# TensorE in program order for the gated delta rule's and the attention's small products, in few groups

## The chip, the cores and the metric

The kernel runs on one core of a Trainium2 chip. The metric is the device time of one execution, in microseconds (us): 2460.8 us before, the median of three runs.

## What is computed

The reference is a two-layer trunk on x of 256 tokens by 2048 channels in fp32. Layer one mixes tokens with a gated delta rule of 16 heads in chunks of 64, layer two with differential attention of 8 heads; each is followed by a feed-forward block (FFN) with a causal convolution of its gate.

```python
# layer 1: projections, convolution, rule, gated norm, output projection
proj = h @ w_in                                   # q, k, v, z, and the gates b, a
qkv = silu(causal_dwconv(proj[..., :o_qkv], conv_w))
beta = sigmoid(b); g = -exp(a_log) * softplus(a + dt_bias)
# in each chunk of 64: decay = exp(g_i - g_j), lower = (beta k) k^T * decay (strictly lower)
sol = triangular_solve(lower, [v * beta, kb * exp(g)], unit_diagonal=True)
# state carried over the chunks; o = q*exp(g) @ state + (q k^T * decay) @ v_new
return (rmsnorm(o, norm_w) * silu(z)) @ w_out
# layer 2: per head two score maps, masked softmax, a = p0 - lam * p1, o = a @ v, rmsnorm, @ w_o
# FFN: (silu(causal_dwconv(gate) + bias) * up) @ w_down
```

## The kernel before

**Large products.** Each fp32 weight block of 128 x 1024 numbers is loaded by SyncE's queue into a tile raw, and split into a high part hi (ScalarE, L219) and a low part lo (VectorE, L220), so that TensorE can take both as fp32r. Such a block is called a half here. Where the weights are stationary (`wstat`: k, q, v heads, FFN, attention's q and k), TensorE runs pairs: hi against 512 columns (L241) and lo against 256 (L242), 8 pairs a half. Where x is stationary (`xstat`, `xstat_steps`: the gate z, w_out, attention's v and w_o, the FFN's second matrix) it runs three products of 512 columns for each of two k blocks and two token tiles (L318 to L320). raw, hi and lo have four buffers each. Four PSUM buffers (mm) hold large results, four (ax) small ones.

**Small products** stand between the large ones:
- gates and decays (`gates_and_decays`): a transpose of the gates (bgT), then for each quarter of the heads three products d1, d2, d3 of 512 columns (L711, L713, L715), whose exponentials ScalarE writes into the tiles ma1 and ma2;
- key products kk (L614, L615) of each head, which VectorE multiplies into ma and reduces to the norms ssk (L618 to L620); from all 16 heads' norms comes cc (L547 to L549), which is transposed (cT_ps, L555). GpSimd then inverts 128 units of 32 x 32 (`eliminate`) and writes them to DRAM (ut_d, un_d), from where 14 copies of 64 KB bring them into the tiles T128 (named t in the trace; L769, L772);
- query products kq and transposes qt (L627 to L632);
- `merge` builds the inverse of 128 x 128 from the 32 x 32 units: 64 products iw, 96 ix, 64 iy (L792, two records of the trace each). `wstat` takes one group of four of them from the list `side` after each k block (`beside`, SMALL = 4);
- rule heads (`head`, `head_end`): per head a chain of transposes and products with ScalarE, VectorE and GpSimd between (L852 to L885), two heads under way;
- attention: scores, transposes of the weights at, products with v (po), transposes aot of the outputs.

**What sets the order.** The program gives each engine's instructions an order in code; the Tile scheduler then orders each engine's queue by its own plan. SyncE's queue and the three compute engines stand in written order only where `manual_schedule` is named (the entry of each block: `in_order`). In the delta rule and the attention TensorE's order is the scheduler's.

Of the kernel before, what the change touches and what calls it, by code (L numbers as in the profile page):

```python
# [15 lines left out]
P = 128  # L16
# [6 lines left out]
AH = 8  # L23
# [9 lines left out]
KEY_LAG, MERGE_AT, HOME_AT = 8, 11, 8  # L33
SMALL = 4
# [68 lines left out]

class Trunk:
    def __init__(self, nc, tc, a, out, cst, stp, bigp, resp, tmp, mmp, axp, scr):
        self.nc, self.tc, self.a, self.out = nc, tc, a, out
        self.cst, self.stp, self.bigp, self.resp, self.tmp = cst, stp, bigp, resp, tmp
        self.mmp, self.axp, self.scr = mmp, axp, scr
        self.due, self.ahead, self.side = [], [], []
# [113 lines left out]
    def wstat(self, srcs, xT, name, early=0):  # L223
# [4 lines left out]
        for hf in range(2):  # L228
# [3 lines left out]
            for k, tt in todo:  # L232
# [10 lines left out]
                self.beside()  # L243
        return ps

    def beside(self):

        if self.side:
            self.side.pop(0)()

    def wstats(self, srcs, xT, first, name):

        for o in self.wstat([srcs[i] for i in range(first)], xT, f"{name}_f", EARLY):
# [211 lines left out]
    def gdn(self):  # L465
# [35 lines left out]
        beta = self.gates_and_decays(gate, ma1, ma2, szt)  # L501
# [9 lines left out]
        late = []  # L511

        def lagging(lag, most, fn, *args):

            late.append((fn, args))
            for _ in range(most):
                if len(late) > lag:
                    f, x = late.pop(0)
                    f(*x)

        def drain():
            while late:
                f, x = late.pop(0)
                f(*x)

        def key_products(h):
            self.key_products(h, K, MA1, MA2, g)
            if h % 4 == 3:
                self.units_out(h // 4, ma1, ma2)
# [6 lines left out]
        z = self.xstat_steps(Blocks(a["w_in"], 48), KD, xT, evac_z, "z")  # L536
        for h in range(NH):
# [11 lines left out]
        nc.vector.tensor_tensor(cc, cc, beta, op=ALU.mult)  # L549
# [14 lines left out]
        self.eliminate(cT, T128, units)  # L564
        self.rsqrt(fl(rb), fl(g["ssk"]), 1.0)
        nc.gpsimd.tensor_tensor(rb, rb, beta, op=ALU.mult)

        for h in range(NH):
            if h == MERGE_AT:
                self.merge(ma1, ma2, cc, T128, units)  # L570
            ps = self.wstat([a["w_in"][h]], xT, f"q{h}")[0]
            qT = self.t([P, S], f"qT{h}", "vT", bufs=3)
            self.conv_silu(qT, ps, h)
            lagging(LAG, 1, self.query_products, h, qT, K, MA1, MA2, g)
            for _ in range(2 - h % 2):
                next(z)
# [4 lines left out]
        vs, heads = [], []  # L581
        for h in range(NH):
            ps = self.wstat([a["w_in"][32 + h]], xT, f"v{h}")[0]
            if h == 0:
                drain()
                self.rsqrt(fl(rq), fl(g["ssq"]), 1.0)
                nc.gpsimd.tensor_scalar(rq, rq, P ** -0.5, None, op0=ALU.mult)
                assert not self.side
            vT = self.t([P, S], f"vT{h}", "vT", bufs=3)
            self.conv_silu(vT, ps, 32 + h)  # L590
            vs.append((h, vT))
            if len(vs) > 1:
                heads.append(self.head(*vs.pop(0), MA1, MA2, T128, negc, rb, rq))
            if len(heads) > 1:
                self.head_end(*heads.pop(0), SZ, oT)
            if h == HOME_AT:
                for tt in range(2):
                    for q in range(4):
                        self.after_halves(tt * 8 + q * 2, lambda tt=tt, sl=slice(q * 512, (q + 1) * 512): nc.sync.dma_start(
                            self.h[:, tt, sl], a["x"][tt * P:(tt + 1) * P, sl]))  # L600
        heads.append(self.head(*vs.pop(0), MA1, MA2, T128, negc, rb, rq))
        for i, x in enumerate(heads):
            self.after_halves(1 + 2 * i, lambda x=x: self.head_end(*x, SZ, oT))
# [18 lines left out]
    def query_products(self, h, q, K, MA1, MA2, g):  # L622

        nc = self.nc
        k, m1, m2 = K[h], MA1[h], MA2[h]
        pp = self.ax(f"kq_{h}")
        nc.tensor.matmul(pp[:, 0:S], k[:, 0:P], q, start=True, stop=True)  # L627
        nc.tensor.matmul(pp[:, S:384], k[:, P:S], q[:, P:S], start=True, stop=True)
        pq = self.ax(f"qt_{h}")
        for p in range(2):  # L630
            qt = pq[:, p * P:(p + 1) * P]
            nc.tensor.transpose(qt, q[:, p * P:(p + 1) * P], self.ident)  # L632
            junk = self.t([P, P], f"jq{h}{p}", "jq")
            nc.scalar.activation(junk, qt, AF.Square, accum_out=g["ssq"][:, p, h:h + 1])
        nc.vector.tensor_tensor(m1[:, 1, :], pp[:, 0:S], m1[:, 1, :], op=ALU.mult)
        nc.vector.tensor_tensor(m2[:, 1, :], pp[:, S:384], m2[:, 1, :], op=ALU.mult)
# [12 lines left out]
    def gates_and_decays(self, ps, ma1, ma2, szt):  # L649
# [22 lines left out]
        xa = self.t([P, S], "ba_xa", "vT", bufs=3)  # L672
# [19 lines left out]
        pt = self.ax("bgT_ps")  # L692
        for p in range(2):
            nc.tensor.transpose(pt[:, p * 64:(p + 1) * 64], bg[0:64, p * P:(p + 1) * P], self.ident[0:64, 0:64])
        bgT = self.cst.tile([P, 2, 64], F32, name="bgT")
        nc.vector.tensor_copy(bgT, pt[:, 0:128].rearrange("p (a c) -> p a c", a=2))
# [3 lines left out]
        for q in range(4):  # L700
# [26 lines left out]
        return bgT[:, :, 0:NH]  # L727
# [14 lines left out]
    def eliminate(self, cT, T128, room):  # L742
# [22 lines left out]
        for p in range(2):  # L765
            for b in range(4):
                u = slice((p * 4 + b) * NH, (p * 4 + b + 1) * NH)
                bs = slice(b * 32, (b + 1) * 32)
                nc.gpsimd.dma_start(T128[p][bs, :, bs], ut[u].rearrange("h c i -> c h i"))  # L769
                if b < 3:  # L770
                    o = (b * 32 + 64) % 128
                    nc.gpsimd.dma_start(T128[p][bs, :, o:o + 32], un[u].rearrange("h i c -> i h c"))  # L772

    def merge(self, ma1, ma2, cc, T128, room):
# [9 lines left out]
        todo = self.side  # L784

        def small(fns):

            for i in range(0, len(fns), SMALL):
                todo.append(lambda part=fns[i:i + SMALL]: [f() for f in part])

        def prod(o, x, y):
            return lambda: nc.tensor.matmul(o(), x(), y(), start=True, stop=True)  # L792

        def quarters(p):
            t = T128[p]
            box = {}

            def begin():
                box[1] = self.ax(f"iw{p}").rearrange("p (h i) -> p h i", h=NH)
                box[2] = self.ax(f"ix{p}").rearrange("p (h i) -> p h i", h=NH)  # L800

            todo.append(begin)
            ws = room[:, p * 512:(p + 1) * 512].rearrange("p (h i) -> p h i", h=NH)
            A, B = (slice(0, 32), slice(64, 96)), (slice(32, 64), slice(96, 128))
            small([
                prod(lambda b=b, h=h: box[1][b, h, :], lambda a=a, b=b, h=h: mt(p, h)[a, b], lambda a=a, h=h, o=o: t[a, h, o:o + 32])
                for h in range(NH) for a, b, o in ((A[0], B[0], 64), (A[1], B[1], 0))])

            def scaled():
                for b in B:  # L810
# [294 lines left out]
```

## Time and profile before

| | us |
|---|---|
| median of three runs (2459.75 to 2467.18) | 2460.8 |
| the profiled execution's own time | 2446.62 |
| its span | 2444.9 |
| TensorE busy in it | 2417.2 |
| VectorE busy | 1654.3 |
| ScalarE busy | 1203.0 |
| GpSimd busy | 148.8 |
| granted TensorE clock, mean | 0.997 |

The profiled execution took 14.2 us less than the median of the timed runs. In the profile the stages follow one another: entry to 45 us, key heads with gates, decays and the first z blocks to 165, query heads with z (and the elimination on GpSimd) to 365, v heads with the rule heads to 495, w_out to 572, FFN to 1300, attention to 1700, FFN to the end. [...]

### The profile page before, as it was taken

How to read it: one execution, taken by the hardware profiler on the slowest of the kernel's cores; microseconds unless marked ns; L12 is line 12 of the kernel's file. 1: busy time of each engine (PE TensorE's matmuls, PEld its weight loads, DVE VectorE, ACT ScalarE, POOL GpSimd, SP SyncE). 2: the span in 40 equal slices, each digit the busy share in tenths (PEclk: the TensorE clock that was granted, in tenths of full speed). 3: DMA queues.
4: the chain of work that ended last, by engine and by line, in shares of the span. 5: the costliest groups of instructions: out<-in, count | busy, mean ns of one | idle time of the engine just before them, and what ended most of it. 6: DMA issues, size and time to landing. Idle time of an engine off the chain costs nothing.

```text
span 2444.9 us, 35002 instructions
## 1 busy us (share of the span) xinstructions
PE 2417.2 (99%) x13203; PEld 2062.2 (84%) x13203; DVE 1654.3 (68%) x2555; ACT 1203.0 (49%) x1940; POOL 148.8 (6%) x237
## 2 busy tenths in 40 slices
PE   9999999999999999999999999999999999999998
PEld 7788778878888888888888888888888888888887
DVE  7777558857877777764446677556777777774444
ACT  6745435545544444444446555444644444444442
POOL 0238201100000000000000000000000000000000
PEclk9999999999999999999999999999999999999999
DMA  6355535444555555565554554455555555555554
GB/s 231 128 176 183 169 113 181 178 159 157 196 190 190 190 190 190 190 209 194 193 195 152 189 185 164 167 189 179 180 190 190 190 189 189 190 195 203 196 193 153
DMA packets 137433, 445.28 MB, mean 182 GB/s; under 512 B 14752, under 2 KB 31952, under 8 KB 136752
## 3 DMA queue, kind: packets, MB, share of 16 engines
q1 hardware_dynamic: 135264, 440.00, 53.1%
q0 software_dynamic: 2000, 3.05, 0.4%
q8 instruction: 103, 1.69, 0.3%
q14 instruction: 66, 0.54, 0.1%
HBM read 439.31 MB, written 3.69 MB: 181 GB/s over the span
## 4 chain that ended last, share of the span: by engine, by line
PE 90%; POOL 3%; issue 2%; ACT 2%; DVE 2%; DMA 1%; SPq 0%; POOLq 0%; DVEq 0%; ACTq 0%
PE ps_up L241 26%; PE ps_up L242 13%; PE ps_d L319 7%; PE ps_d L318 7%; PE ps_d L320 7%; PE ps_v L241 2%; PE ps_ak L241 2%; PE ps_aq L241 2%; PE ps_v L242 1%; PE ps_av L320 1%; PE ps_av L318 1%; PE ps_av L319 1%; PE ps_ao L318 1%; PE ps_ao L319 1%; PE ps_ao L320 1%
## 5 line engine op out<-in xcount | busy, mean ns | idle before, releaser
L241 PE MATMUL ps_up<-xT_f,hi_up 128*128 128x512 f32 x2752 | 955.1, 393 | 0.0
L242 PE MATMUL ps_up<-xT_f,lo_up 128*128 128x256 f32 x2752 | 762.4, 277 | 1.6 <-DVE lo_up L220 1.6
L241 PEld LDWEIGHTS ps_up<-xT_f,hi_up 128*128 128x128 f32 x2752 | 515.9, 187 | 119.0
L219 ACT CAST hi_up<-raw_up 128x1024 fp32r<-128x1024 f32 x344 | 361.1, 1051 | 473.1 <-issue 321.2
L220 DVE TENSOR_TENSOR lo_up<-raw_up,hi_up 128x1024 fp32r<-128x1024 f32 x344 | 421.1, 1225 | 193.7 <-ACT hi_up L219 193.4
L242 PEld LDWEIGHTS ps_up<-xT_f,lo_up 128*128 128x128 f32 x2752 | 516.8, 188 | 3.0 <-DVE lo_up L220 2.7
L220 DVE TENSOR_TENSOR lo_d<-raw_d,hi_d 128x1024 fp32r<-128x1024 f32 x168 | 205.8, 1225 | 223.9 <-ACT hi_d L219 223.9
L219 ACT CAST hi_d<-raw_d 128x1024 fp32r<-128x1024 f32 x168 | 177.1, 1054 | 256.2 <-PE ps_d L320 239.6
L318 PE MATMUL ps_d<-hi_d,hT 128*128 128x512 f32 x672 | 261.4, 389 | 0.0
L320 PE MATMUL ps_d<-hi_d,hT 128*128 128x512 f32 x672 | 261.4, 389 | 0.0
L319 PE MATMUL ps_d<-lo_d,hT 128*128 128x512 f32 x672 | 261.4, 389 | 0.0
L318 PEld LDWEIGHTS ps_d<-hi_d,hT 128*128 128x128 f32 x672 | 126.2, 188 | 26.4
L320 PEld LDWEIGHTS ps_d<-hi_d,hT 128*128 128x128 f32 x672 | 126.1, 188 | 26.3
L319 PEld LDWEIGHTS ps_d<-lo_d,hT 128*128 128x128 f32 x672 | 126.1, 188 | 25.8
L241 PE MATMUL ps_q<-xT_in,hi_q 128*128 128x512 f32 x256 | 97.9, 415 | 0.0
L187 POOL TENSOR_SCALAR qr<-q 128x1 f32<-128x1 f32 x8 | 1.5, 191 | 1578.2 <-DVE q L445 1578.2
L241 PE MATMUL ps_v<-xT_in,hi_v 128*128 128x512 f32 x256 | 93.1, 400 | 0.0
L241 PE MATMUL ps_ak<-xT_kv,hi_ak 128*128 128x512 f32 x240 | 86.8, 402 | 0.0
L901 DVE SCALAR_TENSOR_TENSOR gy<-gs,c_fconv,gy 128x255 f32<-128x255 f32 (+1 forms) x176 | 84.6, 481 | 2.8
L241 PE MATMUL ps_k<-xT_in,hi_k 128*128 128x512 f32 x224 | 81.0, 404 | 0.8 <-DVE s L263 0.8
L646 DVE SCALAR_TENSOR_TENSOR y<-s,c_gconv,y 128x255 f32<-128x255 f32 x144 | 72.2, 502 | 13.9 <-ACT y L644 11.7
L241 PE MATMUL ps_aq<-xT_q,hi_aq 128*128 128x512 f32 x224 | 78.2, 391 | 0.0
(394 smaller groups left out, 4145.0 us busy)
## 6 DMA issues: line engine op xcount, KB each, us to landing
raw_up<-in_w_up SPq DMA_DIRECT2D x344, 512.0 KB, 4.3
raw_d<-in_w_dn SPq DMA_DIRECT2D x176, 512.0 KB, 3.4
raw_z<-in_w_in SPq DMA_DIRECT2D x32, 512.0 KB, 3.9
raw_q<-in_w_in SPq DMA_DIRECT2D x32, 512.0 KB, 3.3
raw_v<-in_w_in SPq DMA_DIRECT2D x32, 512.0 KB, 3.2
raw_wo<-in_w_out SPq DMA_DIRECT2D x32, 512.0 KB, 3.3
raw_av<-in_w_v SPq DMA_DIRECT2D x32, 512.0 KB, 3.3
raw_ao<-in_w_o SPq DMA_DIRECT2D x32, 512.0 KB, 3.2
```

Of the source, the lines that this page charges most:

```text
L187: nc.gpsimd.tensor_scalar(dst, src, scale, EPS, op0=ALU.mult, op1=ALU.add)
L219: nc.scalar.copy(hi[:, c], raw[:, c])
L220: nc.vector.tensor_tensor(lo[:, c], raw[:, c], hi[:, c].bitcast(F32), op=ALU.subtract)
L241: nc.tensor.matmul(to, hi[:, w], x, start=(k == 0 and tt != 1), stop=False)
L242: nc.tensor.matmul(lt, lo[:, w], lx, start=False, stop=(k == KD - 1))
L318: nc.tensor.matmul(to, xh, wh, start=(k == 0), stop=False)
L319: nc.tensor.matmul(to, xh, wl, start=False, stop=False)
L320: nc.tensor.matmul(to, xl, wh, start=False, stop=(k == nk - 1))
L646: nc.vector.scalar_tensor_tensor(y[:, j:S], s[:, 0:S - j], w[:, ct, 3 - j:4 - j], y[:, j:S], op0=ALU.mult, op1=ALU.add)
L901: nc.vector.scalar_tensor_tensor(y[:, j:S], s[:, 0:S - j], w[:, l, f, 2 - j:3 - j], y[:, j:S], op0=ALU.mult, op1=ALU.add)
```

## The change

TensorE's order in the delta rule's heads (`gdn_heads`) and in the attention (`attend_all`) becomes that of the program, by a `manual_schedule` on TensorE alone, and the program is written so that small products stand in few groups:
- bgT after the key head 7, the four quarters of decays around the z blocks of heads 8 and 9, key products of three heads at a time after the z blocks of heads 10 to 14, those of heads 14 and 15 with cT_ps directly behind the query head 0;
- query products of two heads at a time;
- the merge in four runs (iw, ix, two iy), one after each of the query heads 13, 14 and 15 and one at v head 0; the list `side` goes;
- the 14 copies into T128 go from GpSimd's queue to SyncE's, at query head 11 and two halves on;
- a six-stage pipeline of rule heads (class Heads): each step issues one stage of six heads, in three ax buffers; after the last v head six more steps, one half apart, in w_out. The loads of x that are needed again come later for the second token tile;
- attention: scores of a head pair together, the transposes of a head only with the scores of the next, products with v and their transposes for two heads together; the first key head is no longer taken in two token tiles (early 0).

```diff
+    def pe_in_order(self):
+        return self.tc.manual_schedule(engines={mybir.EngineType.PE})
...
-        beta = self.gates_and_decays(gate, ma1, ma2, szt)
+        with self.pe_in_order():
+            self.gdn_heads(gate, ks, xT, ma1, ma2, szt, MA1, MA2, SZ)
+    def gdn_heads(self, gate, ks, xT, ma1, ma2, szt, MA1, MA2, SZ):
+        bg, decays = self.gates_and_decays(gate, ma1, ma2, szt)
...
+        groups = {(7, 0): bg, (8, 0): lambda: decays(0), (8, 1): lambda: decays(1), (9, 0): lambda: decays(2), (9, 1): lambda: decays(3)}
+        for i, hs in enumerate(((0, 1, 2), (3, 4, 5), (6, 7, 8), (9, 10, 11), (12, 13))):
+            groups[10 + i, 1] = lambda hs=hs: key_group(*hs)
         for h in range(NH):
...
             self.conv_silu(K[h], ks[h], 16 + h)
-            lagging(max(1, min(KEY_LAG, 2 * (NH - 1 - h))), 3, key_products, h)
+            groups.get((h, 0), lambda: None)()
             if h >= NH // 2:
                 next(z)
-        drain()
+            groups.get((h, 1), lambda: None)()
+        q0 = self.wstat([a["w_in"][0]], xT, "q0")[0]
+        key_group(14, 15)
...
-        self.eliminate(cT, T128, units)
+        back = self.eliminate(cT, T128, units)
...
         for h in range(NH):
-            if h == MERGE_AT:
-                self.merge(ma1, ma2, cc, T128, units)
+            if h == BACK_AT:
+                back[0]()
+                self.after_halves(2, back[1])
...
+            next(z)
+            if len(late) == 2:
+                self.query_products(late, K, MA1, MA2, g)
+                late = []
+            late.append((h, qT))
+            if h > BACK_AT + 1:
+                next(merge)
+            if h % 2 == 0:
                 next(z)
...
-                nc.gpsimd.dma_start(T128[p][bs, :, bs], ut[u].rearrange("h c i -> c h i"))
+                nc.sync.dma_start(T128[p][bs, :, bs], ut[u].rearrange("h c i -> c h i"))
...
+class Heads:
+    DEPTH = 6
+    def step(self, new):
+        self.under_way = [{"h": new[0], "vT": new[1]} if new else None] + self.under_way[:-1]
+        at = [x for x in enumerate(self.under_way) if x[1]]
+        if not at:
+            return
+        ps = [self.k.ax(f"px{at[0][1]['h']}_{i}") for i in range(3)]
+        room = [ps[0][:, 0:256], ps[0][:, 256:384], ps[0][:, 384:512], ps[1][:, 256:384], ps[1][:, 0:256], ps[2][:, 0:256]]
+        for i, x in reversed(at):
+            (self.turn, self.first, self.across, self.second, self.outputs, self.finish)[i](x, room[i])
...
+        for i in range(pipe.DEPTH):
+            self.after_halves(1 + i, lambda x=last if i == 0 else None: pipe.step(x))
...
-        for c, ps in enumerate(self.wstats(a["w_k"], xkv, 1, "ak")):
+        for c, ps in enumerate(self.wstats(a["w_k"], xkv, 1, "ak", 0)):
             self.add_halves(kq[c][:, 0, :], ps, f"ak{c}")
-            if c % 2 == 1:
-                self.after_halves(2, lambda h=c // 2: self.weights_of(h, kq, aT[h]))
+            if c % 2 == 0 and c > 0:
+                turn()
+                turn = self.weights_of(c // 2 - 1, kq, aT[c // 2 - 1])
```

The three places where the order matters below are shown in rows of each engine's queue. First TensorE at the merge, of the kernel before, in the query head 11: iw products stand in fours behind each pair of large ones (t128 is T128, ma1 the products' tile of the first token tile).

```order
L241 MATMUL ps_q11_0_2834<-xT_in_0_132,hi_q11_0_0_2837 128x512
L242 MATMUL ps_q11_0_2834<-xT_in_0_132,lo_q11_0_0_2838 128x256
L792 MATMUL iw0_2843<-t128_0_1641,ma1_1_386 32x32 x4
L241 MATMUL ps_q11_0_2834<-xT_in_1_151,hi_q11_0_0_2837 128x512
L242 MATMUL ps_q11_0_2834<-xT_in_1_151,lo_q11_0_0_2838 128x256
L792 MATMUL iw0_2843<-t128_0_1641,ma1_1_386 32x32 x4
```

The same products on TensorE of the changed kernel, between the z block that follows query head 13 and query head 14:

```order
L383 MATMUL ps_z_3_1_2798<-hi_z_3_4_3081,xT_in_2_170 128x512
L871 MATMUL iw0_3097<-t128_0_1688,ma1_0_385 32x32 x8
L871 MATMUL iw0_3097<-t128_0_1688,ma1_1_386 32x32 x8
L871 MATMUL iw0_3097<-t128_0_1688,ma1_2_387 32x32 x8
L871 MATMUL iw0_3097<-t128_0_1688,ma1_3_388 32x32 x8
L871 MATMUL iw1_3132<-t128_1_1689,ma2_0_389 32x32 x16
L871 MATMUL iw1_3132<-t128_1_1689,ma2_1_390 32x32 x16
L310 MATMUL ps_q14_0_3167<-xT_in_0_132,hi_q14_0_0_3170 128x512
```

All 64 iw products stand in one run. Counted over the whole order, the 224 products of the merge stood in 48 runs (36 of 32 x 32 products, 12 of 64 x 64) and now stand in 4 (64 iw, 96 ix, 32 iy, 32 iy).

The second place is the transpose cT_ps on TensorE. Before, the last key product (kk_15) stands in the query head 1, and cT_ps 39 rows behind it, after the rest of that head and three quarters of a z block:

```order
L614 MATMUL kk_15_1620<-h_80 128x256
L615 MATMUL kk_15_1620<-h_80 128x128
L242 MATMUL ps_q1_0_1866<-xT_in_0_132,lo_q1_0_0_1870 128x256
...
L320 MATMUL ps_z_1_1_1829<-hi_z_1_2_1937,xT_in_1_151 128x512
L555 MATMUL cT_ps_1644<-ident_81,cc_499 32x128
```

In the changed kernel it is the row behind kk_15, and the z block waits behind it:

```order
L687 MATMUL kk_14_1658<-h_80 128x256
L688 MATMUL kk_14_1658<-h_80 128x128
L687 MATMUL kk_15_1667<-h_80 128x256
L688 MATMUL kk_15_1667<-h_80 128x128
L619 MATMUL cT_ps_1691<-ident_81,cc_429 32x128
L381 MATMUL ps_z_1_0_1816<-hi_z_1_0_1820,xT_in_0_132 128x512
```

VectorE's queue of the changed kernel at that place, where cc is made; it is what cT_ps turns:

```order
L691 SCALAR_TENSOR_TENSOR jd14_1661,ssk_427<-kk_14_1658,ident_81 128x128
L691 SCALAR_TENSOR_TENSOR jd14_1663,ssk_427<-kk_14_1658,ident_81 128x128
L692 TENSOR_TENSOR ma1_3_388<-kk_14_1658,ma1_3_388 128x256
L693 TENSOR_TENSOR ma2_1_390<-kk_14_1658,ma2_1_390 128x128
L289 TENSOR_TENSOR lo_q1_0_1_1880<-raw_q1_0_1_1877,hi_q1_0_1_1879 128x1024
L326 TENSOR_TENSOR s0_1805<-ps_q0_0_1613,c_qkv0_1806 128x256
...
L693 TENSOR_TENSOR ma2_1_390<-kk_15_1667,ma2_1_390 128x128
L328 TENSOR_TENSOR s0_1805<-s0_1805,rb_in_229 128x256
L611 TENSOR_SCALAR cc_429<-ssk_427 128x32
L612 RECIPROCAL cc_429<-cc_429 128x32
L613 TENSOR_TENSOR cc_429<-cc_429,bgT_425 128x32
```

Between the two heads' four operations stand a split of a weight half (lo_q1) and an addition for query head 0 (s0).

## Rows read from the trace of the kernel before

**Rows 1.** The page, part 1: busy time, share of the span and instructions of each engine.

```profile
PE 2417.2 (99%) x13203; PEld 2062.2 (84%) x13203; DVE 1654.3 (68%) x2555; ACT 1203.0 (49%) x1940; POOL 148.8 (6%) x237
```

**Rows 2.** Stretches: start:end, length, busy us of each engine, PEclk, DMA share, GB/s.

```profile
90.00:100.00 10.00, 7.53 (x37) 6.33 (x35) 5.10 (x13) 9.89 (x15) 4.62 (x6) 0.83 0.31 107
250.00:300.00 50.00, 45.85 (x333) 36.45 (x331) 29.34 (x43) 20.91 (x42) 11.65 (x16) 0.93 0.54 174
291.00:298.50 7.50, 4.92 (x63) 4.09 (x64) 1.58 (x5) 1.53 (x4) 1.63 (x3) 0.54 0.22 67
490.00:500.00 10.00, 8.62 (x52) 7.18 (x51) 3.25 (x11) 3.15 (x15) 2.12 (x6) 1.00 0.00 1
500.00:510.00 10.00, 8.53 (x44) 6.18 (x43) 6.20 (x11) 6.89 (x16) 2.12 (x6) 1.00 0.18 57
1500.00:1550.00 50.00, 50.00 (x246) 41.94 (x246) 31.47 (x57) 25.06 (x48) 1.78 (x4) 1.00 0.49 167
```

**Rows 3.** TensorE in order of time, 293 to 298 us: start, length, instruction, [idle before].

```profile
293.58 1.45 PE L792 MATMUL ix<-t,units 32*32 32x32 f32 x46 [4.15 <-DMA t<-ut_d]
294.96 0.80 PE L628 MATMUL kq<-qT,h 128*128 128x128 f32 x2
...
295.62 0.78 PE L318 MATMUL ps_z<-hi_z,xT_in 128*128 128x512 f32 x1
...
297.82 0.43 PE L792 MATMUL ix<-t,units 32*32 32x32 f32 x8
```

**Rows 4.** TensorE in order of time, merge among query heads.

```profile
304.34 0.50 PE L241 MATMUL ps_q<-xT_in,hi_q 128*128 128x512 f32 x1
...
305.13 0.50 PE L241 MATMUL ps_q<-xT_in,hi_q 128*128 128x512 f32 x1
...
336.05 0.50 PE L241 MATMUL ps_q<-xT_in,hi_q 128*128 128x512 f32 x1
...
337.20 0.49 PE L241 MATMUL ps_q<-xT_in,hi_q 128*128 128x512 f32 x1
337.63 1.14 PE L792 MATMUL iy<-t,units 64*64 64x64 f32 x16
338.70 0.39 PE L242 MATMUL ps_q<-xT_in,lo_q 128*128 128x256 f32 x1
```

**Rows 5.** TensorE in order of time, first key product.

```profile
94.09 1.22 PE L614 MATMUL kk<-h 128*128 128x256 f32 x2 [2.47 <-ACT ma L724]
...
97.30 0.40 PE L241 MATMUL ps_k<-xT_in,hi_k 128*128 128x512 f32 x1
...
97.65 0.40 PE L241 MATMUL ps_k<-xT_in,hi_k 128*128 128x512 f32 x1
```

**Rows 6.** ScalarE's groups of instructions, 60 to 101 us: xcount, busy us, mean ns.

```profile
L720 ACT ACT_TABLE_LOAD x4 | 5.1, 1283 | 0.1
```

**Rows 7.** VectorE in order of time, where cc is made.

```profile
171.31 1.23 DVE L220 TENSOR_TENSOR lo_q<-raw_q,hi_q 128x1024 fp32r<-128x1024 f32 x1
172.46 0.28 DVE L618 SCALAR_TENSOR_TENSOR jd<-kk,ident 128x128 f32<-128x128 f32 x1
...
172.88 0.42 DVE L619 TENSOR_TENSOR ma<-kk,ma 128x256 f32<-128x256 f32 x1
...
173.41 0.23 DVE L547 TENSOR_SCALAR cc<-ssk 128x32 f32<-128x32 f32 x1
...
174.29 0.18 DVE L550 TENSOR_SCALAR negc<-cc 128x32 f32<-128x32 f32 x1
```

**Rows 8.** TensorE in order of time, last rule heads.

```profile
494.68 0.39 PE L867 MATMUL px<-x,ma 128*128 128x128 f32 x2
...
498.28 0.44 PE L882 MATMUL px<-ident,on 128*128 128x128 f32 x2 [0.69 <-DVE on L880]
```

**Rows 9.** DMA, 250 to 305 us: queue, share of 16 engines; issues, median us to landing.

```profile
q0 software_dynamic: 736, 1.97, 11.8%
...
t<-ut_d POOLq DMA_DIRECT2D x8, 64.0 KB, 2.8
```

More of the change, by code (lines that the diff above doesn't have):

```diff
@@ L108, in __init__ @@
         self.mmp, self.axp, self.scr = mmp, axp, scr
-        self.due, self.ahead, self.side = [], [], []
+        self.due, self.ahead = [], []
     def q(self, name, dtype=F32):
@@ L242, in wstat, with wstats @@
                     nc.tensor.matmul(lt, lo[:, w], lx, start=False, stop=(k == KD - 1))
-                self.beside()
         return ps
[L246 to L253, printed above, removed]
+    def wstats(self, srcs, xT, first, name, early=EARLY):
+        for o in self.wstat([srcs[i] for i in range(first)], xT, f"{name}_f", early):
             yield o
@@ L510, in gdn, with key_group @@
         K = [self.h[:, h // 8, (h % 8) * S:(h % 8 + 1) * S] for h in range(NH)]
[L511 to L529, printed above, removed]
+        def key_group(*heads):
+            for h in heads:
+                self.key_products(h, K, MA1, MA2, g)
+                if h % 4 == 3:
+                    self.units_out(h // 4, ma1, ma2)
         r = self.r
@@ L764, in eliminate, with back @@
         nc.gpsimd.dma_start(un, tu)
-        for p in range(2):
+        def back(p):
             for b in range(4):
@@ L782, in mt @@
             return ms[h // n].rearrange("p (h a i) -> p h a i", h=n, a=2)[:, h % n, 0, :]
[L784 to L789, printed above, removed]
         def prod(o, x, y):
-            return lambda: nc.tensor.matmul(o(), x(), y(), start=True, stop=True)
-        def quarters(p):
+            nc.tensor.matmul(o, x, y, start=True, stop=True)
+        A, B = (slice(0, 32), slice(64, 96)), (slice(32, 64), slice(96, 128))
@@ L795, in quarters @@
+        quarters = []
+        for p in range(2):
             t = T128[p]
[L796 to L802, printed above, removed]
-            ws = room[:, p * 512:(p + 1) * 512].rearrange("p (h i) -> p h i", h=NH)
[L804 to L807, printed above, removed]
@@ new lines, in merge @@
+            quarters.append(ws)
+        yield
+        for p, ws in enumerate(quarters):
+            t = T128[p]
+            w2 = self.ax(f"ix{p}").rearrange("p (h i) -> p h i", h=NH)
+            for h in range(NH):
+                for a, b in zip(A, B):
+                    prod(w2[a, h, :], ws[b, h, :], t[b, h, b])
+            for h in range(NH):
+                prod(w2[B[0], h, :], t[B[0], h, B[0]], ws[B[0], h, :])
+            for a, b in zip(A, B):
+                nc.vector.tensor_scalar(t[a, :, b], w2[a], -1.0, None, op0=ALU.mult)
+            nc.vector.tensor_scalar(t[B[0], :, 64:96], w2[B[0]], -1.0, None, op0=ALU.mult)
+            nc.gpsimd.memset(t[A[1], :, 0:32], 0.0)
@@ new lines, in merge @@
+                w = self.ax(f"iy{p}{i}").rearrange("p (h i) -> p h i", h=8)
+                for h in range(8):
+                    prod(w[b, h, :], mt(p, i * 8 + h)[a, b], t[a, i * 8 + h, b])
+                ws = room[:, at:at + 512].rearrange("p (h i) -> p h i", h=8)
+                nc.vector.tensor_tensor(ws[b], w[b], cc[b, p, hs].unsqueeze(2).to_broadcast([64, 8, 64]), op=ALU.mult)
+                halves.append((t, hs, ws, w, i))
+        yield
+        for t, hs, ws, w, i in halves:
+            for h in range(8):
+                prod(w[a, h, :], ws[b, h, :], t[b, i * 8 + h, b])
+            nc.vector.tensor_scalar(t[a, hs, b], w[a], -1.0, None, op0=ALU.mult)
@@ L935, in attention, with last_weights @@
         r = self.r
+        def last_weights():
+            turn()
+            ends.append(self.weights_of(AH - 1, kq, aT[AH - 1]))
         def evac_v(nb, tt, ps):
@@ L952, in weights_of @@
         pm, rs = [], self.t([P, 2, 2], f"rs{h}", "rs4")
-        for m in range(2):
-            c = 2 * h + m
+        scores = []
+        for c in (2 * h, 2 * h + 1):
             ps = self.ax(f"sc{c}")
```

304 lines of the change are left out of this document (160 added, 144 removed).

## The prediction

> **What bounds the kernel now.** I read the busy times of the engines first. TensorE is busy 2417.2 us of a span of 2444.9, 99% [rows 1]; no other engine comes near, so only time on TensorE counts: products that take longer than their columns need, waits, and stretches at the lower clock. The FFN, three fifths of the run, is not touched. Next I read stretches. In attention, 1500 to 1550 us, TensorE is busy for all of its 50.00 us at clock 1.00 [rows 2]: nothing to win by filling gaps there. In the delta rule it isn't: 45.85 of 50 us from 250 to 300, 7.53 of 10 us from 90 to 100, and 8.62 and 8.53 of 10 us on both sides of 500 us [rows 2]. Those places, and the many small products between 275 and 361 us, are what the change can touch.
>
> **The change part by part.** All sums are against the profiled execution's 2446.6 us. It lies 14.2 us under the median of the timed runs, so I carry over the difference, not the level.
>
> *Merge in 4 runs instead of 48.* While iw products are spread out, a pair of large products and a group of four small ones (eight records) take 305.13 - 304.34 = 0.79 us [rows 4]; an undisturbed pair takes 97.65 - 97.30 = 0.35 us [rows 5]. A group thus costs 0.44 us. In a long run, 46 records take 294.96 - 293.58 = 1.38 us [rows 3], 0.030 us each, or 0.24 us for eight. The interruption itself is worth 0.20 us. The 36 groups of 32 x 32 products become two runs: 34 x 0.20 = 6.8 us. For the 64 x 64 products, pair and group take 337.20 - 336.05 = 1.15 us [rows 4], so a group of eight records costs 0.80, and all 128 records in eights would cost 12.8 us; a run of sixteen takes 338.70 - 337.63 = 1.07 us [rows 4], 0.067 a record, so 128 would cost 8.6 us in long runs. Some of the 12 groups hold sixteen or more already, and 0.067 still contains the entry into a run; I take 4 us. Together **-10.8 us**, bounds -7 (the lone 64 x 64 saving gone, and a run of 32 x 32 entering and leaving at a price not seen) and -13. I place no gain on grouping key products, decays or attention's products: they are 128 wide like the large ones, and the stretch of attention without gaps, where they stand alone, shows no loss [rows 2].
>
> *The 14 copies into T128 leave GpSimd's queue.* [...] From 294.96 to 297.82 [rows 3] TensorE does columns at half speed, 2.86 us, half of which, 1.4 us, is lost. On SyncE's queue the copies follow weight loads that run up to eight halves ahead of TensorE (four raw buffers, four split ones), 8 x 8 pairs x 0.35 = 22 us. Their own place in the program, two query heads ahead of the first iw product, leaves them as much again. The two waits go: **-5.6 us**; bounds 0 and -5.6. What the copies cost the weights' queue is a rival below.
>
> *Decays and first key products.* At 94.09 TensorE waits 2.47 us for a decay's exponential on ScalarE [rows 5], which is busy 9.89 of 10 us there [rows 2] and loads its function tables again for each change between exponential and silu, 1.28 us a time [rows 6]. Behind it products run at the lower clock up to 97.30 [rows 5]: half of 3.21 us, 1.6 us. The change puts the first key products after key head 10, some 10 us later, and quarters of decays where several halves of large products lie between; ScalarE then has fewer changes of table to make. But in program order each quarter must wait for ax buffers that ScalarE still reads, with nothing to overtake it. Of 4.1 us I take back 3: **-3 us**, bounds 0 and -4.1.
>
> *cT_ps behind kk_15.* This is the new wait. Between kk_14 and cT_ps VectorE has: kk_14's four operations, 173.41 - 172.46 = 0.95 us; the split of a weight half, 172.46 - 171.31 = 1.15; an addition of 128 x 256, at most the 0.42 us that the like-shaped L619 takes; kk_15's four, 0.95; one more such operation, 0.42; and cc, 174.29 - 173.41 = 0.88 [rows 7]. That is 4.77 us. TensorE's share of work beside it is kk_15 alone, some 0.6 us (half of the 1.22 us that such a product's two records took at the lower clock [rows 5]). It waits 4.1 us, with the z block queued behind. Before, 39 rows of large products lay in this place and hid the whole chain. The two waits of this size in the trace, 2.47 and 4.15 us, were both followed by the lower clock, at 1.6 and 1.4 us; I add 1.5: **+5.6 us**, bounds +3 (no fall of the clock, the split done ahead) and +8.
>
> *Rule heads.* While v heads run, a step has the time of a whole head, two halves, 2 x 8 x 0.35 = 5.6 us and its small products, ahead of the next; a stage needs a product and one or two operations. Nothing to win or lose there. At the end TensorE idles 1.38 + 1.47 us in the two stretches around 500 us [rows 2], at full clock. There the outputs' chain takes from the last product at 494.68 to the transposes at 498.28 [rows 8], 3.6 us, with two heads' squares on ScalarE in turn. [...] Of 2.85 us idle and about as much again in split groups I expect 2 back: **-2 us**, bounds -4 and +2.
>
> *Attention.* Transposes and ends move by whole halves, later than the chains of the trace need, and nothing idles now [rows 2]: 0, bounds -1 and +3. The home loads and the ax buffers of the later part are put at 0 too: SyncE's queue has its DMA engines half free there (share 0.49) [rows 2].
>
> *Clock in long runs.* No run of small products in this trace is longer than 46 records, and that one began at the lower clock, so whether 192 records of 32 x 32 products hold the upper level isn't shown. In the run nothing would be lost, since 0.030 us was the price at the lower level; behind each it costs 1.5 us as above. Four runs: 0 to +6, I take **+1.5**.
>
> Sum: -10.8 - 5.6 - 3 + 5.6 - 2 + 0 + 1.5 = -14.3 us. That is 2432.3 us profiled, and 2460.8 - 14.3 = **2446.5 us** on the median.
>
> **Rivals.**
>
> *A, more.* cT_ps waits less and the clock stays up, decays give back everything: 5.6 falls to 3, 3 grows to 4.1, the runs cost nothing: -10.8 - 5.6 - 4.1 + 3 - 2 = -19.5 us, 2441 us. For it: without the split and the addition in the chain, the wait would be 4.77 - 1.57 - 0.6 = 2.6 us. Against: VectorE's order is fixed, and both stand inside.
>
> *B, the clock falls at every run.* Then +6 instead of +1.5: -9.8 us, 2451 us. In the rows the lower clock stands only behind idle time, which speaks against it. [...]
>
> *C, program order stalls everywhere a little.* Each place where the scheduler let a large product overtake now waits: decays give nothing back (0), the last rule heads neither, the merge's four runs wait for VectorE's scaling by 0.5 us each, and the clock takes 1.5 more: -10.8 - 5.6 + 5.6 + 2 + 1.5 + 1.5 = -5.8 us, 2455 us, within what is no change. For it: TensorE was busy at every small product because something else could go first. Against: the written order leaves halves of 2.8 us between most of them.
>
> *D, slower: the copies hold up the weights.* A copy landed 2.8 us after its issue [rows 9], and a queue that takes them one after another would be held 14 x 3 = 42 us. The weights' lead of 22 us would be used up, and TensorE would miss 20 us near query head 12, with the clock lower behind it by 1.5: -14.3 + 21.5 = +7 us, 2468 us. It decides against the change once a copy holds the queue longer than (22 + 14.3) / 14 = 2.6 us. Against it: all transfers of GpSimd's queue from 250 to 305 us, two of 512 KB among them, took 11.8% of 16 engines' time [rows 9], 6.5 us, so less than 0.5 us a copy when spread. [...]
>
> **How the numbers follow.** The sum as forecast has a chance of 0.52; A 0.13, B 0.09, C 0.17, D 0.06 and a stall that I haven't seen (of the rule heads' steps or attention's groups, 22 steps by 1 us or more) 0.03. A measurement of this kernel can tell about 0.3%, 7.4 us, from no change, so faster ends at 2453.4 us. Forecast, A and B are faster, 0.74; C is no change, 0.17; D and the unseen stall slower, 0.09. The range goes from 2437 (A with the merge and the rule heads at their bounds, 2441 - 2 - 2) to 2460 (C with cT_ps at its bound and the merge 3 us short, 2455 + 2.4 + 3); beyond it lies the best end of A, and D. The likeliest case alone, with its bounds, spans 2440 to 2453.
>
> **What would show it.** In the profile after: 4 runs of merge products at about 0.03 and 0.06 us a record with no idle beside; no wait for t on DMA; a wait of 4 us ahead of cT_ps for cc on VectorE, and PEclk near 0.6 for some us behind it; no wait of 2.5 us at the first key product; idle ahead of the last transposes of at most 0.6 us a step; attention's rows at 50.00 of 50. The prediction is wrong if TensorE waits for lo or hi near query head 12 (D), if PEclk falls behind merge runs (B), or if waits in gates, keys and heads come to more than 7 us (C).

## The result, and the profile after

The changed kernel takes **2547.35 us** (median of four runs, 2545.28 to 2547.77) against 2463.99 for the kernel before (2459.75 to 2470.56): ratio 1.0334, 95% interval 1.0307 to 1.0361. It is 3.3% slower, where 0.6% faster was forecast. The profiled execution has a span of 2546.0 us.

The page of the changed kernel, parts 1 and 2, answers to [rows 1]: TensorE is busy for 38 us more, and idle for 63 us more (2546.0 - 2455.2 = 90.8, before 27.7), and the clock falls in the seventh to ninth of 40 slices. PEclk is the granted TensorE clock: in this line in tenths of full speed, in a stretch as a share of it. The lower clock is a PEclk of 0.50: us by us, the first profile of before has 0.50 from 292 to 298 and 1.00 from 299 to 301.

```profile
PE 2455.2 (96%) x13187; PEld 2090.7 (82%) x13187; DVE 1657.9 (65%) x2555; ACT 1198.8 (47%) x1936; POOL 134.8 (5%) x223
...
PEclk9999998889999999999999999999999999999999
```

Stretches of the changed kernel (columns as in [rows 2], PEclk the third from the end):

```profile
250.00:300.00 50.00, 50.00 (x266) 42.87 (x265) 33.13 (x51) 26.67 (x54) 0.00 (x0) 1.00 0.69 206
...
327.00:331.00 4.00, 4.00 (x13) 3.13 (x12) 2.87 (x5) 0.42 (x1) 0.00 (x0) 0.57 0.01 4
400.00:450.00 50.00, 35.44 (x174) 29.78 (x172) 21.14 (x41) 17.65 (x43) 3.25 (x9) 0.83 0.24 84
500.00:550.00 50.00, 33.08 (x166) 27.53 (x165) 21.35 (x44) 16.73 (x43) 4.33 (x12) 0.88 0.26 95
800.00:850.00 50.00, 50.00 (x285) 43.40 (x284) 37.52 (x60) 23.91 (x36) 0.00 (x0) 1.00 0.54 184
1600.00:1650.00 50.00, 50.00 (x236) 41.76 (x235) 30.61 (x50) 24.58 (x44) 1.78 (x4) 1.00 0.48 165
```

The stretch from 250 to 300 us that lost 4.15 us before [rows 2] is full. The loss stands where v heads run. There TensorE works 35 of 50 us, at a clock of 0.83.

By stage, from the starts of the tiles' first products in both traces: the first product for v comes at 343.8 us, before at 363.7 (-19.9); from there to the FFN's first product 316.4 us, before 211.9 (+104.5); attention 388.3, before 390.1 (-1.8); and the first matrix of each FFN 504.8 us, before 495.8 (+18.0 for both, in code that isn't changed). The sum is +100.8, the spans' difference 101.1. The first two figures are not quite like for like: a run of 64 iy records and the last two heads' query products, 5.6 us from 349.61 to 355.25, now stand behind the first v product. Up to there some 14.3 us are won, and the stage behind it lost some 99.

TensorE's waits from 360 to 590 us of the changed kernel (engine, tile and line that waited, what for: us in all, times, longest):

```profile
PE px L144 <- DVE on L162: 51.0, 15, 3.4
PE px L135 <- DVE h L141: 7.3, 15, 1.0
PE px L130 <- ACT h L136: 5.9, 14, 0.6
```

One step of the pipeline on TensorE, in order of time: L167 is the stage finish, L153 the last product of outputs, then second (L144), across (L140), first (L135), turn (L130), each for another head; behind it the next v head.

```profile
433.93 0.38 PE L167 MATMUL px<-ident,on 128*128 128x128 f32 x2
...
434.59 0.39 PE L153 MATMUL px<-h,ma 128*128 128x128 f32 x2
438.43 0.49 PE L144 MATMUL px<-h,t 128*128 128x128 f32 x2 [3.44 <-DVE on L162]
438.75 0.39 PE L140 MATMUL px<-h,ma 128*128 128x128 f32 x2
439.60 0.49 PE L135 MATMUL px<-h,t 128*128 128x128 f32 x2 [0.46 <-DVE h L141]
440.65 0.69 PE L130 MATMUL px<-ident,vT 128*128 128x128 f32 x2 [0.56 <-ACT h L136]
440.99 0.78 PE L310 MATMUL ps_v<-xT_in,hi_v 128*128 128x512 f32 x1
...
441.78 0.63 PE L310 MATMUL ps_v<-xT_in,hi_v 128*128 128x512 f32 x1
...
442.42 0.63 PE L310 MATMUL ps_v<-xT_in,hi_v 128*128 128x512 f32 x1
...
443.64 0.39 PE L310 MATMUL ps_v<-xT_in,hi_v 128*128 128x512 f32 x1
...
443.99 0.39 PE L310 MATMUL ps_v<-xT_in,hi_v 128*128 128x512 f32 x1
```

The product second (L144) has nothing to do with the value on (L162) for which it waits: on is made from the outputs of another head. What they share is the PSUM buffer px1, whose columns 0 to 255 hold outputs and 256 to 383 second. So the wait goes by buffer here and not by column: L144 waits 51.0 us in all for readers of other columns, and with outputs in a buffer of their own that wait is gone (the first experiment). In the same way first (L135) waits for the reader of across, 7.3 us, and turn (L130) for that of first, 5.9 us, all three in px0. outputs has the slowest readers of the three: squares, a root on GpSimd, and on itself; second starts only 3.84 us after L153. A pair that takes 0.35 us (443.99 - 443.64) takes 0.64 behind the wait (442.42 - 441.78), at the lower clock (0.50 from 441 to 443). Between 396 and 584 us the clock is down to 0.50 14 times, for some 3 to 7 us each.

### The profile page after: what moved, and what is told of

The parts are those of the page before. It is cut to its first block, busy times and chain, and to the rows that moved or that the text cites. A ratio compares the mean times of both kernels' runs of the same rounds, so it can differ in the third digit from the quotient of the medians.

```text
span 2546.0 us, 34970 instructions
## 1 busy us (share of the span) xinstructions
PE 2455.2 (96%) x13187; PEld 2090.7 (82%) x13187; DVE 1657.9 (65%) x2555; ACT 1198.8 (47%) x1936; POOL 134.8 (5%) x223
## 4 chain that ended last, share of the span: by engine, by line
PE 92%; DVE 3%; ACT 2%; issue 1%; POOL 1%; DMA 0%; SPq 0%; POOLq 0%; DVEq 0%; ACTq 0%
PE ps_up L310 25%; PE ps_up L311 13%; PE ps_d L383 6%; PE ps_d L381 6%; PE ps_d L382 6%; PE ps_v L310 3%; PE ps_q L310 2%; PE ps_ak L310 2%; PE ps_aq L310 2%; PE ps_v L311 1%; PE ps_wo L381 1%; PE ps_wo L382 1%; PE ps_wo L383 1%; PE ps_q L311 1%; PE ps_z L381 1%; PE ps_k L310 1%
## 5 line engine op out<-in xcount | busy, mean ns | idle before, releaser
L310 PE MATMUL ps_up<-xT_f,hi_up 128*128 128x512 f32 x2752 | 973.2, 399 | 0.0
L311 PE MATMUL ps_up<-xT_f,lo_up 128*128 128x256 f32 x2752 | 772.7, 281 | 1.6 <-DVE lo_up L289 1.6
L310 PE MATMUL ps_v<-xT_in,hi_v 128*128 128x512 f32 x256 | 105.5, 447 | 0.0
L310 PE MATMUL ps_q<-xT_in,hi_q 128*128 128x512 f32 x256 | 91.1, 398 | 0.0
L289 DVE TENSOR_TENSOR lo_v<-raw_v,hi_v 128x1024 fp32r<-128x1024 f32 x32 | 39.2, 1225 | 61.4 <-ACT hi_v L288 61.2
```

Source lines behind the costliest of these rows:

```text
L289: nc.vector.tensor_tensor(lo[:, c], raw[:, c], hi[:, c].bitcast(F32), op=ALU.subtract)
L310: nc.tensor.matmul(to, hi[:, w], x, start=(k == 0 and tt != 1), stop=False)
L311: nc.tensor.matmul(lt, lo[:, w], lx, start=False, stop=(k == KD - 1))
```

## The experiments

**The outputs in a buffer of their own.**

```diff
-        ps = [self.k.ax(f"px{at[0][1]['h']}_{i}") for i in range(3)]
-        room = [..., ps[1][:, 256:384], ps[1][:, 0:256], ps[2][:, 0:256]]
+        ps = [self.k.ax(f"px{at[0][1]['h']}_{i}") for i in range(4)]
+        room = [..., ps[1][:, 256:384], ps[3][:, 0:256], ps[2][:, 0:256]]
```

> The changed kernel, with the outputs' products of a rule head's step in a fourth ax buffer of their own, not in that of the stage second. Theory: each of the 15 steps idles because products of different heads share a PSUM buffer, and the next product into a buffer waits until all earlier results in it are read; the wait of 3.44 us for the outputs' readers ahead of the stage second (51.0 us in all) then goes nearly whole, the two shorter ones (7.3 and 7.4 us) stay, and with less idle time the lower clock goes too: 51 to 70 us less, a span of 2475 to 2495. Rival 1, the chain of one head is too long for its step (its own data come late): the wait moves to another product and less than 10 us is won. Rival 2, program order as such: the same, less than 10 us.

Measured: 2474.81 us, span 2473.1, 72.9 less than the changed kernel's and just below my range. (9.0 of it is the pace of one FFN, see the end.) TensorE's waits from 350 to 520 us of this kernel:

```profile
PE px L135 <- DVE h L141: 20.3, 15, 1.5
PE px L130 <- ACT h L136: 5.0, 14, 0.4
```

The wait of L144 is gone whole. The two at the buffer that is still shared stay, and that of L135 has grown by 13.0 us, so part of the 51.0 has moved, as rival 1 said of its wait. But some 64 us are won, not less than 10: both rivals fall.

**A buffer for each stage, the step in two halves.**

```diff
+        self.some((5, 3, 4))                      # finish, second, outputs
+        if new and later:
+            self.k.after_halves(1, lambda: self.some((2, 1, 0)))
+        else:
+            self.some((2, 1, 0))                  # across, first, turn
...
+                c = self.k.ax(f"px{i}_{x['h']}")[:, 0:width[i]]
```

> The changed kernel, with each stage's products in an ax buffer of its own and a step of the rule heads cut in two, finish, second and outputs ahead of a v head's first half, across, first and turn ahead of its second. TensorE stays in program order. Theory (shared buffers): all waits of the v heads' stage go, 66 us of idle and some 25 us of lower clock: 80 to 95 us less than the changed kernel, 2452 to 2467 us, a ratio of 0.995 to 1.002 to the kernel before. Rival 1 (the chain is too long): 20 us or less. Rival 2 (program order as such makes the steps wait): 20 us or less.

Each stage's products take the next of the four ax buffers in turn. Measured: 2439.31 us, ratio 0.992 (0.9892 to 0.9948) to the kernel before, 108 less than the changed kernel: more than was expected of the theory, 99.0 of it between first v product and FFN (217.4 us) and 9.0 in one FFN. Buffers and half steps changed together here; the run before changed a buffer alone. A stretch of it that answers to the one of 35.44 us:

```profile
400.00:450.00 50.00, 50.00 (x330) 45.37 (x329) 40.55 (x91) 31.74 (x84) 9.48 (x21) 1.00 0.49 154
```

TensorE is still in program order here. Program order alone, then, costs next to nothing in the v heads: the run after next has them in the scheduler's order and takes 215.4 us for the same stage.

**The v heads in the scheduler's order, buffers shared.** The `with self.pe_in_order()` ends before the first v head.

> The changed kernel, with TensorE in program order only up to the last query head; v heads, the six-stage pipeline and w_out in the scheduler's order. Shared buffers stay. Theory: the waits themselves remain, but large products can go first, so much of the 90 us comes back, 40 to 85 us less, if the scheduler's plan knows of the waits. Rival 2 (program order is the whole cause): all of it, 85 to 95 us. Rival 1 (chain too long): nothing comes back, since the next step needs the chain.

Measured: 2445.74 us, span 2444.0, 102 less than the changed kernel's, 9 of it an FFN's pace. Between first v product and FFN it takes 224.1 us, 6.6 more than with own buffers. I had set 40 to 85 for my theory and 85 to 95 for the rival; some 93 is in the rival's range. So the loss needs both, shared buffers and a queue that nothing may overtake, and undoing either is enough. That is more than my theory said.

**The rule heads of before behind the changed front part.** `head` and `head_end` come back, and the scheduler's order from the first v head.

> The changed kernel with the rule heads of the kernel before (two under way, one buffer a head, the scheduler's order from the first v head on); gates, decays, keys, queries, merge, the copies and the attention as changed. By my sum for these parts (-10.8 - 5.6 - 3 + 5.6 + 1.5 = -12.3) the time is 2449 to 2455 us, ratio 0.994 to 0.997; by the traces, in which the first v head starts some 16 us earlier like for like, 2446 to 2450, ratio about 0.993. Rival: if the front part only shifted work into the v heads, the ratio is 0.999 or more.

Measured: 2438.13 us, ratio 0.9917 (0.9886 to 0.9948), below both of my ranges, and with one FFN at the slower pace. Without the new rule heads the change is thus 0.8% faster, where 0.6% was forecast of the whole. That what it won came from where the forecast placed it doesn't follow from this run; see the merge below.

**cT_ps two z blocks later** (in the kernel with half steps).

```diff
             if h % 2 == 0:
                 next(z)
+            if h == 0:
+                back = invert()      # cT_ps, uc, eliminate, as they stood ahead of the loop
```

> The kernel with steps in two halves, with the transpose cT_ps (and the elimination behind it) two z blocks later, so that 24 large products stand between the last key product and it. Theory (the 2.73 us of wait at cT_ps and the lower clock behind it come from program order alone, and the elimination has that much time to spare): 2.7 us of idle and about 1.4 of lower clock less, 4 us, 2435 us, ratio 0.990 to the kernel before. Rival: the later elimination makes the copies or the first iw products wait: no gain, 2439 or more.

Measured: 2425.61 us, ratio **0.9881** (0.9854 to 0.9908), the fastest kernel here but for its twins below. Of the 13.7 us to the kernel with half steps 9.0 are an FFN's pace; the first v product comes at 337.9, there at 343.4. From the first query product to it are 181.3 us, there 185.9: 4.6 less, for which 4 was expected. TensorE of this kernel at the place:

```profile
170.02 0.39 PE L390 MATMUL ps_z<-hi_z,xT_in 128*128 128x512 f32 x1
170.25 0.27 PE L629 MATMUL cT_ps<-ident,cc 128*32 128x128 f32 x1
170.27 0.47 PE L317 MATMUL ps_q<-xT_in,hi_q 128*128 128x512 f32 x1
```

No wait, and the copies still come in time: TensorE is busy for 50.00 of 50 us from 250 to 300.

**The copies back on GpSimd's queue** (nc.sync.dma_start becomes nc.gpsimd.dma_start in `back`; half steps kept).

> The kernel with steps in two halves, with the 14 copies into T128 back on GpSimd's queue. Prediction's step (-5.6 us for taking them off it): TensorE waits 4 us or more for a copy ahead of the first iw products and the clock falls behind it, 5 us more. Rival: the merge now stands two query heads later than before, and 14 issues 3.3 to 4 us apart are done by then: no wait, and the time is unchanged, so that not the queue but the place of the merge won the 5.6 us.

Measured: 2448.43 us, of which 9.0 us, again, are one FFN's slower pace; the first v product comes at 343.2 us, with SyncE's queue at 343.4. Its stretches around the first iw products:

```profile
250.00:300.00 50.00, 50.00 (x265) 42.89 (x264) 33.19 (x51) 26.67 (x57) 9.20 (x14) 1.00 0.66 204
...
300.00:350.00 50.00, 50.00 (x596) 43.13 (x596) 33.34 (x50) 19.68 (x35) 1.04 (x2) 0.97 0.42 132
```

The copies' issues on GpSimd's queue stand 2.7 to 5.3 us apart, 3.6 in the mean (thirteen from 255.32 to 299.00). The rival holds: with the merge this late there is no wait on either queue, and SyncE's queue wins nothing.

**The kernel before once more.**

> The kernel before, unchanged, profiled once more. In the profile of before both FFN's first matrices took 495.8 us, in the changed kernel's both 504.8, in the four experiments so far one each, with the same instructions. Theory A: which of the two paces a stretch of pairs falls into differs from execution to execution of one kernel; then 495.8 or 504.8 may stand in either FFN here, and the time follows by 9 us each. Theory B: it is fixed by the kernel: 495.8 in both.

Measured: 2461.83 us, 15.2 more than the profile that the prediction rests on. Both FFNs took 495.8 us, so the two theories are not told apart by it. The time went elsewhere; TensorE at the copies' wait, and stretches behind it:

```profile
297.88 1.46 PE L792 MATMUL ix<-t,units 32*32 32x32 f32 x46 [4.75 <-DMA t<-ut_d]
```

```profile
290.00:300.00 10.00, 3.11 (x55) 2.51 (x54) 1.62 (x4) 0.51 (x1) 1.96 (x3) 0.71 0.35 111
300.00:310.00 10.00, 10.00 (x67) 6.71 (x65) 2.72 (x5) 2.10 (x6) 2.48 (x4) 0.50 0.25 74
310.00:320.00 10.00, 10.00 (x70) 6.36 (x69) 3.28 (x4) 1.04 (x1) 0.00 (x0) 0.50 0.16 52
320.00:330.00 10.00, 10.00 (x51) 7.97 (x51) 5.75 (x10) 3.65 (x9) 0.52 (x1) 0.75 0.18 54
```

Here the clock stays at 0.50 for over 20 us behind the wait, though TensorE is busy all the time, with groups of small products between the large ones. In the first profile it was back within 7.5 us [rows 2]. The first v product comes at 377.0, not at 363.7. From the first query product to it are 216.5 us, not 204.7: the query heads hold 11.8 of the 15.2 us between the two profiles.

**One product more in each FFN** (with the later cT_ps).

> The kernel with the later transpose, with one product of 128 columns more (its result unused) in each FFN, ahead of the fifth pair of gate and up blocks. Theory: the pace of the pairs is a rhythm that TensorE falls into and keeps until something breaks it; one short product can then change the pace from there on, 495.8 to 504.8 or back, or in part. Rival: the pace is set by where the tiles lie in memory or by the load of the DMA queues; then the FFNs take the same time as in the kernel without the product.

Measured: 2423.8 us, both FFNs 495.8, as without it. That is what the rival said, but the theory said only that the pace can change, so the two aren't told apart.

**The merge later in the kernel before.**

```diff
-KEY_LAG, MERGE_AT, HOME_AT = 8, 11, 8
-SMALL = 4
+KEY_LAG, MERGE_AT, HOME_AT = 8, 13, 8
+SMALL = 8
```

> The kernel before with two numbers changed: the merge begins at query head 13, not 11, and its products stand in groups of eight, not four (28 groups, not 48). The copies stay on GpSimd's queue, TensorE's order is the scheduler's. In the second profile of before, the wait for the copies was followed by the lower clock for some 30 us, in which the merge's groups stood; the first profile had the clock back after 5. Theory: this stretch, not the number of groups, is most of what the front part of the change wins: no wait for t, no such stretch, 13 to 20 us less than the median of before, ratio 0.991 to 0.995. Rival (what wins is the small number of groups and program order): 20 x 0.2 us of groups and 4 us of wait, 8 us less, ratio 0.9965 or more.

Measured: 2441.99 us, 19.1 less than 2461.1, ratio 0.9912 (0.9879 to 0.9945). Two of its stretches:

```profile
290.00:300.00 10.00, 10.00 (x52) 8.43 (x51) 6.72 (x11) 5.16 (x10) 1.31 (x2) 1.00 0.55 178
300.00:310.00 10.00, 10.00 (x204) 8.00 (x204) 4.98 (x5) 3.43 (x6) 1.95 (x3) 1.00 0.59 175
```

TensorE waits for nothing from 250 us to the first v product, and the lower clock stands there once, for some 3 us (0.83 in the mean from 320 to 330). The FFN's first product comes at 560.6 us, in the changed kernel with the heads of before at 559.7, before at 575.6 and 590.5: two numbers win what the whole front part of the change does.

The range was met, but the place of the merge and the size of its groups changed together, and what each wins stays open. On TensorE the merge stood not in 28 groups but in 13 runs, since the scheduler joined groups. Two rows of one run of 128 records:

```profile
308.09 1.05 PE L792 MATMUL ix<-t,units 32*32 32x32 f32 x55
...
309.06 0.98 PE L792 MATMUL ix<-units,t 32*32 32x32 f32 x26
```

From the first query product to the first v product it takes 188.6 us, 16.1 less than in the first profile of before. Waits and clock are some 5 us of that (4.2 us of idle time are gone, and the clock gave back less than one); the other 11 go with 35 runs less, 0.3 us each. Against the second profile, 27.9 us less, the long stretch at the lower clock weighs more. So the rival counted 20 interruptions less where there were 35 less, and the part of my theory that the number of groups matters little isn't shown.

**The rule heads of before with the later cT_ps.**

> The changed kernel's front part with the transpose cT_ps two z blocks later, and the rule heads of before in the scheduler's order. It differs from the kernel with half steps and the later transpose (2425.6 us) in the rule heads alone. Theory: a pipeline of six stages wins nothing over two heads under way where the scheduler may fill the chain with large products; by the traces from the first v head to the FFN it takes 215.4 us against 217.5: 2421 to 2426 us. Rival: program order wins in the v heads once no buffer is shared: 2430 or more.

Measured: 2432.05 us median, 2424.23 to 2433.40, ratio 0.9865 (0.9822 to 0.9908). The median lies in the rival's range. But in its profile one FFN takes 504.7 us, and from first v product to FFN it takes 215.4 us against 217.4, as the theory said; without that FFN's 9 us it would equal the kernel with half steps. The two kernels with cT_ps in its old place and one slower FFN each, 2438.13 and 2439.31 us, agree with that. The pipeline wins nothing.

**Stages from the youngest head to the oldest** (for i, x in at, not reversed; three shared buffers).

> The changed kernel with one line changed: a step issues its stages from the youngest head to the oldest (turn, first, across, second, outputs, finish), in the same three shared buffers. Theory: a product waits only for the readers of the product ahead of it in its buffer, so the outputs' readers, the slow ones, hold up nobody (the next product in that buffer is a step away), and three waits of 0.4 to 0.8 us remain in each step: some 22 us of idle in place of 66, a span of 2475 to 2500. Rival (three buffers for six stages are too few in any order): 2530 or more.

Measured: 2469.63 us, span 2467.9, both FFNs 495.9: without their share of 18.0 us, 60 less than the changed kernel. A step on TensorE and a stretch:

```profile
474.71 0.49 PE L135 MATMUL px<-h,t 128*128 128x128 f32 x2 [0.70 <-DVE h L132]
475.55 0.49 PE L140 MATMUL px<-h,ma 128*128 128x128 f32 x2 [0.35 <-ACT h L136]
...
476.62 0.49 PE L151 MATMUL px<-h,ma 128*128 128x128 f32 x2 [0.35 <-ACT h L145]
```

```profile
400.00:450.00 50.00, 42.95 (x236) 36.02 (x235) 32.19 (x65) 23.95 (x59) 5.71 (x15) 0.93 0.35 116
```

As expected: three waits of 1.40 us in all, each for the reader of the product ahead in its buffer. My range was met only with the FFNs' 18 us put back.

## Why the prediction was wrong

**The step that failed is "Rule heads": "a stage needs a product and one or two operations. Nothing to win or lose there."** It looked at each head's own chain, which does have a step's time, and not at the buffers: six stages of six heads in three PSUM buffers, issued so that the product behind outputs shares its buffer. The diff showed it (room names ps[1] for second and for outputs), and [rows 8] had the price, 3.6 us from the last product of outputs to the end of its readers. 15 steps by 3.6 would have been 54 us; measured were 51.0 at that place and 64.2 with the two smaller waits. From the first v product to the FFN TensorE idles 66.2 us, in the kernel with half steps 3.8: 62.4 of the 99.0 us between the two. The other 37 are for the most part the lower clock: the mean PEclk of this stage is 0.89, at most 35 of its 316.5 us. "A stall that I haven't seen" had 0.03. Whether the waits at L144, L135 and L130 are needed was not shown: the trace has them, and no run left them out with the buffers shared and the order kept.

**Merge, -10.8.** Right, as far as the traces can part it. In the changed kernel 128 records of iw take 312.73 - 310.59 = 2.14 us, 0.017 each; the 0.030 of [rows 3] was a price at the lower clock. An interruption was thus worth 0.44 - 8 x 0.017 = 0.30 us, not 0.20. A run of 64 iy records takes 3.87. From the first query product to the first v product the changed kernel takes 187.1 us, before 204.7; less the 5.6 us that moved behind, and with idle time and lost clock nearly equal, some 12 us are left for the merge. It is an estimate: no run changed the merge's order alone, and the kernel before with a later merge got nearly the same gain from 13 runs, without program order.

```profile
310.59 2.21 PE L871 MATMUL iw<-t,ma 32*32 32x32 f32 x128
312.73 0.50 PE L310 MATMUL ps_q<-xT_in,hi_q 128*128 128x512 f32 x1
...
339.89 3.94 PE L871 MATMUL iy<-t,ma 64*64 64x64 f32 x64
343.76 0.50 PE L310 MATMUL ps_v<-xT_in,hi_v 128*128 128x512 f32 x1
```

**Copies, -5.6.** The term is the idle time of [rows 3], 4.15 us, and 1.4 us at the lower clock behind it. The wait went, but not by the queue, and it was undersized: the first profile was an execution in which the clock came back soon. In the second the same stage took 11.8 us more. Carrying the difference over from one execution was the error: if the second profile is typical, most of the 14.2 us between the first and the median lay in the stage that the change touched. Rival D didn't happen; 250 to 300 us is full with the copies on either queue.

**cT_ps, +5.6.** Right in size: 1.00 us of wait for key head 15, which the sum didn't have, and 2.73 for cc, together 3.73 for 4.1, and the lower clock behind them (0.50 from 168 to 170). Moving the transpose won 4.6 us; the 1.00 stayed.

```profile
164.09 0.70 PE L687 MATMUL kk<-h 128*128 128x256 f32 x2 [1.00 <-ACT h L724]
...
167.74 0.40 PE L619 MATMUL cT_ps<-ident,cc 128*32 128x128 f32 x1 [2.73 <-DVE cc L613]
...
168.36 0.63 PE L382 MATMUL ps_z<-lo_z,xT_in 128*128 128x512 f32 x1
...
170.73 0.40 PE L382 MATMUL ps_z<-lo_z,xT_in 128*128 128x512 f32 x1
```

**Decays, -3.** 2.47 us of wait at the first key product and 1.6 of lower clock went, a wait of 2.05 us at a z block came, at full clock (1.00 from 78 to 84): 2 us won there. From the first key product to the first query product it takes 128.6 us, before 131.8. **Last rule heads, -2.** No run shows this term, nor the 0.6 us of idle time a step that the forecast allows ahead of the last transposes. Before, w_out's products of 512 columns start 0.227 us apart (twelve in 2.72 us, 510.06 to 512.78). In the changed kernel the last transposes wait once, 0.40 us at 588.22, and the steps in w_out lose 9.9 us in three waits at L144 (560.71, 571.68 and 579.33). **Attention, 0:** -1.8. **Clock in long runs, +1.5:** it fell behind one run of four (0.57 from 327 to 331), for which 1.5 was a fair price, and rival B, a fall behind each, didn't come. That the lower clock stands only behind idle time, as B had it, doesn't hold here (see the end). With the copies on GpSimd's queue the stretch from 300 to 350 us, where the merge begins, has 0.97. **The FFN** was left out as untouched; it cost 18 us against the first profile.

## What to carry to other kernels

Before a queue is put in program order, list for each instruction the readers of whatever shares its PSUM buffer, not its own inputs alone: in a queue that nothing can overtake, the slowest reader in the buffer was a wait for everything behind, 51.0 us here. A buffer of its own for the slow one took that wait away whole, and 64 of the 99 us with it; an order of issue that puts it last in its buffer won 59. And where one profiled execution stands off the median, find out in which stage before a difference is carried over.

## What the runs showed of the hardware

**The lower clock can come, and hold, while TensorE is busy.** In the changed kernel it fell at 327.5 us (1.00 from 326 to 327, 0.50 from 328 to 330), behind the run of 192 ix records; from 310 to 327 TensorE had no idle time:

```profile
310.00:327.00 17.00, 17.00 (x380) 14.97 (x379) 14.25 (x25) 6.85 (x16) 1.04 (x2) 1.00 0.45 157
```

In the second profile of before it was busy for 10.00 of 10 us at a clock of 0.50, twice in a row, with small groups among large products. Whether the groups hold it down wasn't tried by itself; where they stood in other places or in long runs, no stretch as long was seen.

**Pairs had two paces here.** The same products of both FFNs, 2752 pairs and some in two token tiles, took either 495.8 or 504.8 us a matrix: in 50 us 285 products in the changed kernel (800 to 850 us, above), 290 in the second profile of before, of which this is a stretch, both at full clock and without idle time. 504.8 stood twice in the changed kernel and with the copies on GpSimd's queue, 495.8 twice in both profiles of before, with the later cT_ps, with one product more and with stages from the youngest; the other six profiles had one of each. Six runs of the kernel with the later cT_ps (2424.28 to 2426.71 five times, 2434.89 once) suggest that executions of one kernel differ by it. What sets it stays open: one more product of 128 columns did not change it.

```profile
900.00:950.00 50.00, 50.00 (x290) 43.68 (x290) 37.95 (x59) 24.13 (x36) 0.00 (x0) 1.00 0.59 190
```
